# The forget bias of a two-layer attention trunk: four matrix products a head, or a bias tile added by the masking operation

## The chip, the cores and the metric

One core of one Trainium2 chip runs the whole kernel in a single launch. The metric is the device time of that launch in microseconds (us), the median of several executions. TensorE is called PE here, VectorE DVE, ScalarE ACT, GpSimd POOL and SyncE SP; PE's weight loads are PEld.

## The reference

The trunk has two layers over 256 tokens of width 1024. Each layer projects its normalised input and runs three attention branches side by side (MoBA with 6 heads, NSA with 4, FoX with 6, heads of 64), gates them, and projects back. Only the FoX branch matters here. Its logits carry a forget bias, the running sum of a log gate:

```python
log_f = jax.nn.log_sigmoid((ff + b_f)).transpose(0, 2, 1)      # (B, 6 heads, S)
csum = jnp.cumsum(log_f, axis=-1)
s = einsum('bhqd,bhkd->bhqk', q, k) * ATTN_SCALE + cq[..., None] - csum[:, :, None, :]
p = masked_softmax(s, kpos[None, :] <= t[:, None])
```

So each logit of head h gets csum[h, query] - csum[h, key], and keys behind the query's position are masked out.

## The kernel before

The 256 tokens are two tiles of 128. The large products (projections, gates, output) run in three passes on split weights: ACT rounds a staged 128x1024 tile `st` to `wh` (line 275), DVE takes the rest `wl` (line 276), and lines 297 to 299 multiply. Staged tiles have six buffers and split tiles four, so SP loads and ACT/DVE split ahead of PE.

PE's instructions stand in an order that the code writes out itself (`tick`, `unit` and `pairs` weave pieces of attention between the dense products by a clock of their own). The other engines' instructions are put in order by the scheduler of the framework. Each engine then runs its own list strictly in that order and waits on semaphores of the others.

`fz_post` makes the forget sums: a polynomial for the log gate, then three small products with a triangle (lines 880 to 882) that leave csum of the 6 heads on 6 partitions, 256 columns. ACT copies this out (`zf`, line 884), DVE and ACT split it into two parts each of `cpos` and `cneg` (lines 885 to 889), matrices that are zero outside these rows.

`attend` does one head. PE forms the logits of the two query tiles (128 keys for the first, 256 for the second) with two products each (lines 550 and 551). In FoX heads two more products follow for each tile (lines 554 and 555): a column `selr` that picks head h, broadcast, against `cneg`, and `cpos` against the same column. Then DVE adds the mask and takes the row minimum in one operation (line 561, a custom instruction), ACT takes the exponential (line 563), PE transposes (line 568), ACT or DVE copies the transposes out as `pt` (lines 570, 572), and PE multiplies by the values (lines 576 to 580). Heads come in pairs, three FoX pairs a layer. The PSUM tiles `at` of logits, transposes and column layouts share three buffers, so PE's next use of one waits for the engine that reads it last.

Of the kernel before, what the change touches and what calls it, by code (L numbers as in the profile page):

```python
# [9 lines left out]
F32 = mybir.dt.float32  # L10
F32R = mybir.dt.float32r
AF = mybir.ActivationFunctionType
# [6 lines left out]
NT = S // 128  # L19
# [13 lines left out]


K_TRI, K_MASK, K_CMASK, K_CM01 = 0, 128, 384, 448
K_COS, K_SIN, K_CROPE, K_SEL, K_E = 512, 544, 576, 608, 640
K_GCOL, K_PET, K_W2, K_END = 648, 664, 728, 1240

R_G, R_BF, R_NC, R_END = 0, 256, 268, 396

# [1 line left out]
def shape_tables():  # L42
    t = np.arange(S)
    inv = (np.float32(THETA) ** (-np.arange(0, 16, 2, dtype=np.float32) / np.float32(16))).astype(np.float32)

    def rope(pos):
        ang = (pos.astype(np.float32)[:, None] * inv[None, :]).astype(np.float32).astype(np.float64)
        c, s = np.cos(ang), np.sin(ang)
        return (np.concatenate([c, c], 1).astype(np.float32),
                np.concatenate([-s, s], 1).astype(np.float32))  # L50

    k = np.zeros((128, K_GCOL), np.float32)
    i = np.arange(128)
    k[:, K_TRI:K_TRI + 128] = i[:, None] <= i[None, :]
    k[:, K_MASK + 128:K_MASK + 256] = np.where(i[None, :] <= i[:, None], 0.0, NEG)
    end = np.arange(32) * CS + CL - 1
    ok = (end[None, :] <= t[:, None]) & (np.arange(32) < NCMP)[None, :]
    c, s = rope(t)
    for n in range(NT):
        r = slice(n * 128, n * 128 + 128)  # L60
        k[:, K_CMASK + n * 32:K_CMASK + n * 32 + 32] = np.where(ok[r], 0.0, NEG)
        k[:, K_CM01 + n * 32:K_CM01 + n * 32 + 32] = ok[r]
        k[:, K_COS + n * 16:K_COS + n * 16 + 16] = c[r]
        k[:, K_SIN + n * 16:K_SIN + n * 16 + 16] = s[r]
    c, s = rope(end[:NCMP])
    k[:NCMP, K_CROPE:K_CROPE + 16] = c
    k[:NCMP, K_CROPE + 16:K_CROPE + 32] = s
    for kv in range(2):
        for part in range(2):
            for j in range(NCMP):  # L70
                k[(kv * 2 + part) * 16 + j, K_SEL + kv * NCMP + j] = 1.0
    for h in range(FH):
        k[h::32, K_E + h] = 1.0
    return k


# [18 lines left out]
def trunk(ctx, tc, x, w_in, b_gate, cmp_w1, w_up_moba, w_up_nsa, w_up_fox, w_out, first_d, x_t, small_d, row_d, out):  # L95
# [16 lines left out]
    sm = ctx.enter_context(tc.tile_pool(name="sm", bufs=2))  # L112
    pacc = ctx.enter_context(tc.tile_pool(name="pacc", bufs=4, space=PSUM))
    pat = ctx.enter_context(tc.tile_pool(name="pat", bufs=3, space=PSUM))
    po = ctx.enter_context(tc.tile_pool(name="po", bufs=1, space=PSUM))


# [17 lines left out]
    gbc = row[:, R_G:R_BF].rearrange("p (a b) -> p a b", a=16)  # L135
    bfb = row[:, R_BF:R_NC].rearrange("p (l h) -> p l h", l=L)
    ncg = row[:, R_NC:R_END].rearrange("p (l d) -> p l d", l=L)
    selr = const.tile([128, FH], F32R, name="selr")
    cpos = const.tile([128, S], F32R, name="cpos")
    cneg = const.tile([128, S], F32R, name="cneg")  # L140

    klT = {k: const.tile([128, 6, S], F32R, name="klT_" + k) for k in ("mk", "fk")}
    tri = tabs[:, K_TRI:K_TRI + 128]
# [17 lines left out]
    def late_consts():  # L161
        V.memset(ones1, 1.0)
        G.memset(zer, 0.0)
        for s in (0, 64):
            V.memset(gcol[s:s + 16, 0:12], 1.0)
        G.tensor_copy(selr, tabs[:, K_E:K_E + FH])

    def zero_lows():
        for k in klT:
            v = klT[k].rearrange("p (k a) c -> p k a c", a=2)  # L170
            for i in range(2):
                o = slice(64 - i * 64, 128 - i * 64)
                G.tensor_copy(v[o, :, i, :], zer[o][:, :, None].to_broadcast([64, 3, S]))

    def zero_csums():
        G.tensor_copy(cpos, zer.to_broadcast([128, S]))
        G.tensor_copy(cneg, zer.to_broadcast([128, S]))


    nosync = mybir.DependencyInfo(mybir.DependencyClass.NoSync, mybir.DependencyReason.DATA)  # L180
# [181 lines left out]
    def layer(l):  # L362
# [178 lines left out]
        def attend(q, ks, vf, h, bank, hb, rsum, bias=False):  # L541

            wait = in_turn()
            ps = pat.tile([128, 512], F32, name="at")
            p = wk.tile([128, 384], F32, name="p", bufs=4)
            pt = wk.tile([128, 384], F32, name="pt", bufs=3)
            keys = [(t, 128 * (t + 1), ps[:, t * 128:t * 128 + 128 * (t + 1)]) for t in range(NT)]
            for t, nk, sp in keys:
                qs = slice(t * 128, (t + 1) * 128)
                T.matmul(sp, q[:, qs], ks[0][:, 0:nk], start=True, stop=False)  # L550
                T.matmul(sp, q[:, qs], ks[1][:, 0:nk], start=False, stop=not bias)  # L551
                if bias:
                    one = selr[:, h:h + 1]
                    T.matmul(sp, one.to_broadcast([128, 128]), cneg[:, 0:nk], start=False, stop=False)
                    T.matmul(sp, cpos[:, qs], one.to_broadcast([128, nk]), start=False, stop=True)  # L555
                if t < NT - 1:
                    yield None
            for t, nk, sp in keys:
                u = p[:, t * 128:t * 128 + nk]
                nm = sm.tile([128, 1], F32, name="nm", bufs=4)  # L560
                V.tensor_tensor_reduce(out=u, in0=sp, in1=tabs[:, K_MASK + 256 - nk:K_MASK + 256],  # L561
                                       scale=-SCALE, scalar=BIG, op0=ALU.add, op1=ALU.min, accum_out=nm)
                exps.append(A.activation(u, u, AF.Exp, bias=nm, scale=-1.0,  # L563
                                         accum_out=rsum[:, t, hb:hb + 1]))
            yield LAG_S
            pts = pat.tile([128, 512], F32, name="at")
            for s in range(3):
                T.transpose(pts[:, s * 128:(s + 1) * 128], p[:, s * 128:(s + 1) * 128], ident)  # L568
            if h % 2:
                A.activation(pt, pts[:, 0:384], AF.Copy)  # L570
            else:
                V.tensor_copy(pt, pts[:, 0:384])  # L572
            yield LAG_P
            yield from wait(hb == 0)
            bank = bank()
            T.matmul(bank[:, 0, hb, :], pt[:, 0:128], vf(0), start=True, stop=True)
            yield PV
            T.matmul(bank[:, 1, hb, :], pt[:, 128:256], vf(0), start=True, stop=False)
            yield PV
            T.matmul(bank[:, 1, hb, :], pt[:, 256:384], vf(1), start=False, stop=True)  # L580
            turn[1] += 1
# [270 lines left out]
        def fz_post():  # L852
            ps = sh["ps_fz"]
            xf = sm.tile([128, NT, FH], F32, name="xf")
            mn = sm.tile([128, NT, FH], F32, name="mn")
            e = sm.tile([128, NT, FH], F32, name="e")
            d = sm.tile([128, NT, FH], F32, name="d")
            y = sm.tile([128, NT, FH], F32, name="y")
            for t in range(NT):
                V.scalar_tensor_tensor(xf[:, t, :], ps[t][:, 0:FH], sh["r"][:, t:t + 1], bfb[:, l, :],  # L860
                                       op0=ALU.mult, op1=ALU.add)
            V.tensor_scalar(mn, xf, 0.0, None, op0=ALU.min)
            V.scalar_tensor_tensor(e, mn, 2.0, xf, op0=ALU.mult, op1=ALU.subtract)
            exps.append(A.activation(e, e, AF.Exp))
            for t in range(NT):
                evac(ps, t, FH, 384, sh["z"][t][:, 640:1024])

            V.tensor_scalar(d, e, 2.0, None, op0=ALU.add)
            V.reciprocal(d, d)
            V.tensor_tensor(e, e, d, op=ALU.mult)  # L870
            V.tensor_tensor(d, e, e, op=ALU.mult)
            V.tensor_scalar(y, d, 2.0 / 17, 2.0 / 15, op0=ALU.mult, op1=ALU.add)
            for m in (13, 11, 9, 7, 5, 3, 1):
                V.tensor_tensor(y, y, d, op=ALU.mult)
                V.tensor_scalar(y, y, 2.0 / m, None, op0=ALU.add)
            V.tensor_tensor(y, y, e, op=ALU.mult)
            V.tensor_tensor(y, mn, y, op=ALU.subtract)
            yield LAG_F
            ps = pat.tile([128, 512], F32, name="at")
            T.matmul(ps[0:FH, 0:128], y[:, 0, :], tri, start=True, stop=True)  # L880
            T.matmul(ps[0:FH, 128:256], y[:, 0, :], ones1.to_broadcast([128, 128]), start=True, stop=False)
            T.matmul(ps[0:FH, 128:256], y[:, 1, :], tri, start=False, stop=True)
            cs = wk.tile([FH, S], F32, name="zf", bufs=1)
            A.activation(cs, ps[0:FH, 0:S], AF.Copy, scale=1.0 / SCALE)
            V.tensor_copy(cpos[0:FH], cs)
            hi = cpos[0:FH].bitcast(F32)
            V.tensor_tensor(cpos[32:32 + FH], cs, hi, op=ALU.subtract)
            A.activation(cneg[0:FH], hi, AF.Copy, scale=-1.0)
            V.tensor_tensor(cneg[32:32 + FH], hi, cs, op=ALU.subtract)


        def load_gl(c):
# [155 lines left out]
        def run(starts, following):  # L1048
# [9 lines left out]
            mm("mv1")  # L1058
            uv = unit(v_post("mv"))
            if l == 0:  # L1060
                zero_csums()
                zero_lows()
                later_loads()
            mm("b0")
# [94 lines left out]
```

## Time and profile before

| | |
|---|---|
| median of 3 runs | 523.15 us (523.08 to 523.24) |
| profiled execution: its own time | 524.93 us |
| its span, first to last instruction | 522.8 us |
| PE busy | 508.3 us, 97% |
| DVE busy | 395.0 us, 76% |
| ACT busy | 326.3 us, 62% |
| POOL busy | 106.4 us, 20% |
| mean DMA rate | 174 GB/s |

The profiled execution spends 2.1 us outside its span and is 1.8 us above the median; both are kept in mind when a sum is made against it. Busy shares are averages over the whole span and say little about one stage; stretches are read one by one below.

### The profile page before, as it was taken

To read this page: it belongs to the slowest core of one execution; us is meant where nothing else is said; L and a number is where in the kernel's file an instruction comes from. 1 tells how busy PE (TensorE), PEld (TensorE's weight loads), DVE (VectorE), ACT (ScalarE), POOL (GpSimd) and SP (SyncE) were. 2 spreads that over 40 slices of the span, in tenths; PEclk is the share of its full clock that TensorE was granted. 3 is DMA by queue.
4 is the path that set the end of the run, shared out by engine and by line. 5 is a ranking of instruction groups with operands and counts; after the bars stand their busy time and mean duration, and the time that the engine had idled before them with its cause. 6 is when DMAs were issued, how large, how long until landed. Compare 5 with 4: busy or idle time off the path is not lost.

```text
span 522.8 us, 8342 instructions
## 1 busy us (share of the span) xinstructions
PE 508.3 (97%) x2862; PEld 453.4 (87%) x2862; DVE 395.0 (76%) x804; ACT 326.3 (62%) x619; POOL 106.4 (20%) x166
## 2 busy tenths in 40 slices
PE   7999999999999999899999989999999999989997
PEld 4899899999888888788889979999988888878886
DVE  3898787789974558898487987768898754697953
ACT  4886686976584375644276966678756555655440
POOL 3754314000300004025102333030011000132300
PEclk8999999999999999999999989999999999999999
DMA  8998876445554433655447987546437542445502
GB/s 296 334 245 245 234 234 188 141 154 162 173 180 126 147 121 93 205 171 181 136 144 216 226 230 218 178 135 197 158 120 213 170 123 83 160 131 192 180 21 80
DMA packets 56602, 90.73 MB, mean 174 GB/s; under 512 B 3696, under 2 KB 30960, under 8 KB 56560
## 3 DMA queue, kind: packets, MB, share of 16 engines
q1 hardware_dynamic: 55840, 89.08, 56.4%
q10 hardware_dynamic: 720, 1.12, 0.6%
q8 instruction: 22, 0.36, 0.3%
q14 instruction: 20, 0.16, 0.1%
HBM read 89.14 MB, written 1.05 MB: 173 GB/s over the span
## 4 chain that ended last, share of the span: by engine, by line
PE 67%; issue 15%; DVE 7%; POOL 5%; ACT 4%; DMA 1%; ACTq 0%; DVEq 0%; POOLq 0%
PE acc L297 19%; PE acc L299 18%; PE acc L298 18%; DVE wl L276 3%; ACT wh L275 2%; PE at L568 2%; DMA st<-in_w_in_dram 1%; POOL qn L452 1%; DVE om L921 1%; PE at L550 1%; PE at L551 1%; PE at L348 1%; PE at L460 1%; PE o L758 1%; PE o L757 1%
## 5 line engine op out<-in xcount | busy, mean ns | idle before, releaser
L276 DVE TENSOR_TENSOR wl<-st,wh 128x1024 fp32r<-128x1024 f32 (+4 forms) x177 | 201.8, 1147 | 65.3 <-ACT wh L275 63.6
L275 ACT ACTIVATE wh<-st 128x1024 fp32r<-128x1024 f32 (+4 forms) x177 | 169.9, 966 | 98.4 <-PE acc L299 72.0
L297 PE MATMUL acc<-wh,hT 128*128 128x512 f32 (+3 forms) x576 | 223.8, 388 | 2.4 <-ACT wh L275 2.2
L299 PE MATMUL acc<-wh,lT 128*128 128x512 f32 (+3 forms) x576 | 210.4, 365 | 0.0
L298 PE MATMUL acc<-wl,hT 128*128 128x512 f32 (+3 forms) x576 | 209.7, 364 | 0.4 <-DVE wl L276 0.4
L299 PEld LDWEIGHTS acc<-wh,lT 128*128 128x128 f32 x576 | 108.6, 189 | 12.4 <-DVE lT L404 0.9
L297 PEld LDWEIGHTS acc<-wh,hT 128*128 128x128 f32 x576 | 109.4, 190 | 11.0 <-ACT wh L275 2.8
L298 PEld LDWEIGHTS acc<-wl,hT 128*128 128x128 f32 x576 | 109.4, 190 | 8.5 <-DVE wl L276 1.4
L563 ACT ACTIVATE p<-p,nm 128x128 f32<-128x128 f32 x80 | 35.5, 445 | 29.6 <-DVE nm L561 29.5
L920 POOL TENSOR_TENSOR z<-z,tmp 128x512 f32<-128x512 f32 x8 | 13.0, 1653 | 113.2 <-ACT tmp L917 113.2
L561 DVE CUSTOM_DVE_ANT_0 p<-at,tabs 128x128 f32<-128x128 f32 x80 | 24.1, 352 | 9.9 <-PE at L555 9.8
L956 POOL TENSOR_TENSOR mg<-mg,tmp 128x512 f32<-128x512 f32 x8 | 15.8, 1998 | 55.0 <-DVE tmp L955 55.0
L297 PE MATMUL acc<-wh,qkT 128*128 128x512 f32 x64 | 25.2, 394 | 0.0
L299 PE MATMUL acc<-wh,qkT 128*128 128x512 f32 x64 | 24.9, 390 | 0.0
L298 PE MATMUL acc<-wl,qkT 128*128 128x512 f32 x64 | 24.9, 389 | 0.0
L568 PE MATMUL at<-first,p 128*128 128x128 f32 x120 | 19.8, 274 | 0.3 <-ACT qkT L483 0.2
L660 POOL TENSOR_TENSOR om<-om,tmp 128x256 f32<-128x256 f32 x8 | 7.7, 985 | 58.1 <-DVE rs_a L330 50.3
L906 DVE SCALAR_TENSOR_TENSOR gl<-acc,rt,tmp 128x512 f32<-128x512 f32 x24 | 17.0, 743 | 1.1 <-PE o L580 1.1
L568 PEld LDWEIGHTS at<-first,p 128*128 128x128 f32 x120 | 15.0, 146 | 2.5 <-ACT qkT L483 0.6
L758 PE MATMUL o<-wl,Z 128*63 128x256 f32 x64 | 16.3, 289 | 0.9 <-DVE wl L276 0.9
L757 PE MATMUL o<-wh,Z 128*63 128x256 f32 x64 | 16.6, 295 | 0.0
L572 DVE COPY pt<-at 128x384 f32<-128x384 f32 x20 | 11.0, 551 | 7.0 <-PE at L568 6.8
(232 smaller groups left out, 710.0 us busy)
## 6 DMA issues: line engine op xcount, KB each, us to landing
st<-in_w_in_dram SPq DMA_DIRECT2D x54, 512.0 KB, 3.4
st<-in_w_in_dram SPq DMA_DIRECT2D x56, 384.0 KB, 3.9
st<-in_cmp_w_dram SPq DMA_DIRECT2D x32, 256.0 KB, 4.2
st<-in_w_out_dram SPq DMA_DIRECT2D x16, 512.0 KB, 3.8
st<-in_w_in_dram SPq DMA_DIRECT2D x8, 396.0 KB, 6.9
st<-in_w_in_dram SPq DMA_DIRECT2D x8, 390.0 KB, 3.3
tmp<-in_b_gate_dram SPq DMA_DIRECT2D x12, 256.0 KB, 4.4
st<-in_w_up_moba_dram SPq DMA_DIRECT2D x4, 512.0 KB, 3.7
```

Source lines behind the costliest of these rows:

```text
L275: A.activation(h, sv[:, i:i + m], AF.Copy)
L276: V.tensor_tensor(w_["l"][:, i:i + m], sv[:, i:i + m], h.bitcast(F32), op=ALU.subtract)
L297: T.matmul(ps, sh, wh, start=first, stop=False)
L298: T.matmul(ps, sh, wl, start=False, stop=False)
L299: T.matmul(ps, sl, wh, start=False, stop=last)
L561: V.tensor_tensor_reduce(out=u, in0=sp, in1=tabs[:, K_MASK + 256 - nk:K_MASK + 256], scale=-SCALE, scalar=BIG, op0=ALU.add, op1=ALU.min, a ...
L563: exps.append(A.activation(u, u, AF.Exp, bias=nm, scale=-1.0, accum_out=rsum[:, t, hb:hb + 1]))
L568: T.transpose(pts[:, s * 128:(s + 1) * 128], p[:, s * 128:(s + 1) * 128], ident)
L757: T.matmul(U, st, h, start=i == 0, stop=False)
L758: T.matmul(U, st, lo, start=False, stop=i == CL - 1)
L906: V.scalar_tensor_tensor(sh["gl"][t][b][:, n * 512:(n + 1) * 512], ps[t], sh["r"][:, t:t + 1], bg, op0=ALU.mult, op1=ALU.add)
L956: (G if b == 1 else V).tensor_tensor(m, m, tmp, op=ALU.add)
```

## The change

The two extra products for each tile are gone, and with them `selr`, `cpos`, `cneg` and the steps that made them. Instead, ACT scales the 6x256 sums twice (negative and positive), writes them to a buffer in device memory (`csd`), and loads them back from there: once spread over all 128 partitions as key rows (`ck`, two transfers of 128x6x128 and 128x6x256 numbers), and once with queries on the partitions (`cq`, two transfers of 128x6 single numbers). POOL adds the causal mask to the two diagonal blocks of `ck` for all heads at once. For each head and query tile ACT makes a bias tile from `ck` plus the query's own sum (an Identity activation with a bias column), and the masking operation of DVE reads this tile in place of the mask.

```diff
+            if bias:
+                both = wk.tile([128, 384], F32, name="bias", bufs=3)
+                for t, nk, _ in keys:
+                    add[t] = both[:, t * 128:t * 128 + nk]
+                    A.activation(add[t], sh["ck"][:, h, t * 128:t * 128 + nk], AF.Identity, bias=sh["cq"][:, t, h:h + 1])
...
                 T.matmul(sp, q[:, qs], ks[0][:, 0:nk], start=True, stop=False)
-                T.matmul(sp, q[:, qs], ks[1][:, 0:nk], start=False, stop=not bias)
-                if bias:
-                    one = selr[:, h:h + 1]
-                    T.matmul(sp, one.to_broadcast([128, 128]), cneg[:, 0:nk], start=False, stop=False)
-                    T.matmul(sp, cpos[:, qs], one.to_broadcast([128, nk]), start=False, stop=True)
+                T.matmul(sp, q[:, qs], ks[1][:, 0:nk], start=False, stop=True)
...
-                V.tensor_tensor_reduce(out=u, in0=sp, in1=tabs[:, K_MASK + 256 - nk:K_MASK + 256],
+                V.tensor_tensor_reduce(out=u, in0=sp, in1=add[t],
...
-            cs = wk.tile([FH, S], F32, name="zf", bufs=1)
-            A.activation(cs, ps[0:FH, 0:S], AF.Copy, scale=1.0 / SCALE)
-            V.tensor_copy(cpos[0:FH], cs)
-            hi = cpos[0:FH].bitcast(F32)
-            V.tensor_tensor(cpos[32:32 + FH], cs, hi, op=ALU.subtract)
-            A.activation(cneg[0:FH], hi, AF.Copy, scale=-1.0)
-            V.tensor_tensor(cneg[32:32 + FH], hi, cs, op=ALU.subtract)
+
+            cs = wk.tile([FH, 2, S], F32, name="cs", bufs=1)
+            for i in range(2):
+                A.activation(cs[:, i, :], ps[0:FH, 0:S], AF.Copy, scale=(2 * i - 1) / SCALE)
+            csd = dram.tile([FH, 2, S], F32, name="csd")
+            sh["ck"] = lay.tile([128, FH, 384], F32, name="ck")
+            sh["cq"] = lay.tile([128, NT, FH], F32, name="cq")
+            nc.scalar.dma_start(csd, cs)
+            nc.scalar.dma_start(sh["ck"][:, :, 0:128], csd[:, 0, 0:128][None].to_broadcast([128, FH, 128]))
+            nc.scalar.dma_start(sh["ck"][:, :, 128:384], csd[:, 0, :][None].to_broadcast([128, FH, S]))
+            for t in range(NT):
+                nc.scalar.dma_start(sh["cq"][:, t, :], csd[:, 1, t * 128:(t + 1) * 128].rearrange("h q -> q h"))
+            mask = tabs[:, K_MASK + 128:K_MASK + 256][:, None, :].to_broadcast([128, FH, 128])
+            for i in (0, 256):
+                G.tensor_tensor(sh["ck"][:, :, i:i + 128], sh["ck"][:, :, i:i + 128], mask, op=ALU.add)
...
-        G.tensor_copy(selr, tabs[:, K_E:K_E + FH])
...
-                zero_csums()
```

The changed program's lines are numbered differently (the exponential of line 563 is its line 556, the split of 275 its 266); names with a number are buffers. PE's list is the old one with the 48 rows of lines 554 and 555 taken out and nothing else moved. Two places on ACT and one on POOL differ in more than that; the second layer repeats them.

On ACT, where the forget sums leave PSUM in the first layer, there stood before (`uc` is NSA's compressed branch, `rs_y` a normalisation, `p` the exponentials of the first MoBA pair):

```order
L884 ACTIVATE zf_1718<-at_1714 6x256
L830 ACTIVATE uc_1675<-uc_1675 128x128
L275 ACTIVATE wh_1730<-st_1728 128x1024
L327 ACTIVATE rs_y_1693<-rs_v_1692 128x2x6
L888 ACTIVATE cneg_100<-cpos_99 6x256
L328 ACTIVATE rs_y_1693<-rs_y_1693 128x2x6
L563 ACTIVATE p_1752,rsum_1750<-p_1752,nm_1763 128x128
```

In the changed program the same place, up to the same exponential, reads:

```order
L879 ACTIVATE cs_1714<-at_1710 6x256 x2
L883 DMA csd_1717<-cs_1714 6x512
L823 ACTIVATE uc_1671<-uc_1671 128x128
L318 ACTIVATE rs_y_1689<-rs_v_1688 128x2x6
L266 ACTIVATE wh_1733<-st_1731 128x1024
L319 ACTIVATE rs_y_1689<-rs_y_1689 128x2x6
L884 DMA ck_1718<-csd_1717 128x6x128
L885 DMA ck_1718<-csd_1717 128x6x256
L887 DMA cq_1719<-csd_1717 128x6x1 x2
L556 ACTIVATE p_1755,rsum_1753<-p_1755,nm_1766 128x128
```

Five transfer issues have come in; the four loads stand behind a wait for the store to land, and the exponentials of the first MoBA pair stand behind the four loads.

A little later on ACT, between the last exponential of the first MoBA pair and the first of the second, there stood before:

```order
L563 ACTIVATE p_1757,rsum_1750<-p_1757,nm_1774 128x256
L275 ACTIVATE wh_1811<-st_1809 128x1024
L275 ACTIVATE wh_1885<-st_1883 128x1024
L570 ACTIVATE pt_1758<-at_1843 128x384
L563 ACTIVATE p_1849,rsum_1750<-p_1849,nm_1861 128x128
```

and now stands:

```order
L266 ACTIVATE wh_1788<-st_1786 128x1024
L266 ACTIVATE wh_1814<-st_1812 128x1024
L266 ACTIVATE wh_1888<-st_1886 128x1024
L544 ACTIVATE bias_2084<-ck_1718,cq_1719 128x128
L563 ACTIVATE pt_1761<-at_1846 128x384
L544 ACTIVATE bias_2084<-ck_1718,cq_1719 128x256
L544 ACTIVATE bias_2092<-ck_1718,cq_1719 128x128
L544 ACTIVATE bias_2092<-ck_1718,cq_1719 128x256
L544 ACTIVATE bias_2155<-ck_1718,cq_1719 128x128
L544 ACTIVATE bias_2155<-ck_1718,cq_1719 128x256
L556 ACTIVATE p_1852,rsum_1753<-p_1852,nm_1864 128x128
```

Six bias tiles, for the first three of the six FoX heads, now stand there, one ahead of the copy `pt` and five between it and the next exponentials. The other six stand later, in front of the second and third FoX pair.

On POOL, in the same stretch, the second pair of NSA sums `om` stood before behind the first and one fill:

```order
L660 TENSOR_TENSOR om0_115<-om0_115,tmp_1744 128x256
L660 TENSOR_TENSOR om1_116<-om1_116,tmp_1747 128x256
L803 MEMSET vcb_3854 128x256
L660 TENSOR_TENSOR om0_115<-om0_115,tmp_1837 128x256
L660 TENSOR_TENSOR om1_116<-om1_116,tmp_1840 128x256
```

and now has the two mask additions ahead of it:

```order
L653 TENSOR_TENSOR om0_114<-om0_114,tmp_1747 128x256
L653 TENSOR_TENSOR om1_115<-om1_115,tmp_1750 128x256
L890 TENSOR_TENSOR ck_1718<-ck_1718,tabs_96 128x6x128 x2
L796 MEMSET vcb_3851 128x256
L653 TENSOR_TENSOR om0_114<-om0_114,tmp_1840 128x256
L653 TENSOR_TENSOR om1_115<-om1_115,tmp_1843 128x256
```

The first addition waits for the smaller transfer of `ck`, the second for the larger. The first bias tile on ACT waits for the first addition and the first transfer of `cq`, the second for the second addition and the second transfer of `cq`.

## Rows read from the trace of the kernel before

**Rows 1.** The page's head: span, then busy time (share) and instructions of PE.

```profile
span 522.8 us, 8342 instructions
PE 508.3 (97%) x2862; PEld 453.4 (87%) x2862; DVE 395.0 (76%) x804; ACT 326.3 (62%) x619; POOL 106.4 (20%) x166
```

**Rows 2.** Stretches: length, busy PE, PEld, DVE, ACT, POOL, clock, DMA, GB/s.

```profile
140.00:142.00 2.00, 2.00 (x15) 1.78 (x15) 2.00 (x4) 0.40 (x1) 1.52 (x2) 1.00 0.96 332
162.00:183.00 21.00, 21.00 (x137) 18.74 (x136) 10.35 (x31) 9.61 (x25) 0.00 (x0) 1.00 0.41 127
308.00:310.00 2.00, 1.68 (x7) 1.58 (x8) 0.90 (x2) 0.76 (x3) 0.25 (x1) 0.59 1.06 229
```

**Rows 3.** PE's waits in the whole span: us in total, times, longest.

```profile
PE at L348 <- DVE qkT L354: 3.2, 2, 1.6
PE at L460 <- POOL qn L452: 2.7, 4, 1.3
```

**Rows 4.** PE in order of time: start, us; a MoBA pair's logits, then a FoX pair's.

```profile
139.63 0.30 PE L550 MATMUL at<-qkT 128*128 128x128 f32 x1
...
140.63 0.39 PE L297 MATMUL acc<-wh,hT 128*128 128x512 f32 x1
...
161.95 0.31 PE L550 MATMUL at<-qkT 128*128 128x128 f32 x1
...
163.84 0.39 PE L297 MATMUL acc<-wh,hT 128*128 128x512 f32 x1
```

**Rows 5.** Line 554 (line 555 likewise): ns (min/median/max), first and last start.

```profile
L554 PE MATMUL at<-cneg,selr x24: 273/276/281, 162.2 to 438.5; 128*128 128x128 f32 x12, 128*128 128x256 f32 x12
```

**Rows 6.** ACT in order of time where the sums leave PSUM.

```profile
127.43 0.38 ACT L884 ACTIVATE zf<-at 6x256 f32<-6x256 f32 x1
...
129.69 0.20 ACT L328 ACTIVATE rs_y<-rs_y 128x12 f32<-128x12 f32 x1
132.76 0.40 ACT L563 ACTIVATE p<-p,nm 128x128 f32<-128x128 f32 x1 [2.87 <-DVE nm L561]
```

**Rows 7.** Issue times of loads on ACT's queue, ns (min/median/max).

```profile
L256 ACTq DMA_DIRECT2D st<-in_w_in_dram x4: 452/453/631, 1.2 to 2.6; - x4
```

**Rows 8.** Transfers: count, KB each, median us from issue to landing.

```profile
st<-in_w_in_dram SPq DMA_DIRECT2D x54, 512.0 KB, 3.4
...
out_dram<-x SPq DMA_DIRECT2D x2, 128.0 KB, 1.7
```

**Rows 9.** DMA from 158 to 160 us, while one b_gate load runs alone.

```profile
DMA packets 158, 0.29 MB, mean 145 GB/s; under 512 B 16, under 2 KB 16, under 8 KB 158
```

**Rows 10.** Line 897 (b_gate spread over 128 partitions, 256 KB): issue to landing.

```profile
DMA to landing us min/median/max: 3.2/4.4/5.2
```

**Rows 11.** DMA from 16 to 20 us, when many loads run at once.

```profile
DMA packets 1031, 1.50 MB, mean 376 GB/s; under 512 B 60, under 2 KB 1031, under 8 KB 1031
```

**Rows 12.** POOL's additions of 256 and 512 columns, ns (min/median/max).

```profile
L660 POOL TENSOR_TENSOR om<-om,tmp x8: 736/740/1721, 131.7 to 397.4; 128x256 f32<-128x256 f32 x8
L920 POOL TENSOR_TENSOR z<-z,tmp x8: 1301/1744/1827, 199.5 to 460.5; 128x512 f32<-128x512 f32 x8
```

**Rows 13.** ACT in order of time from the last split to the column layouts.

```profile
138.72 1.06 ACT L275 ACTIVATE wh<-st 128x1024 fp32r<-128x1024 f32 x1 [1.75 <-PE acc L299]
139.91 0.49 ACT L570 ACTIVATE pt<-at 128x384 f32<-128x384 f32 x1
142.55 0.40 ACT L563 ACTIVATE p<-p,nm 128x128 f32<-128x128 f32 x1 [2.15 <-DVE nm L561]
```

**Rows 14.** Line 563: exponentials of 128 and 256 columns, ns (min/median/max).

```profile
L563 ACT ACTIVATE p<-p,nm x80: 383/448/510, 91.6 to 440.2; 128x128 f32<-128x128 f32 x40, 128x256 f32<-128x256 f32 x40
```

**Rows 15.** PE's next uses of a freed PSUM buffer, in order of time.

```profile
141.32 0.49 PE L460 MATMUL at<-first,qn 128*128 128x128 f32 x3
...
149.13 0.50 PE L568 MATMUL at<-first,p 128*128 128x128 f32 x3
```

**Rows 16.** DVE in order of time: the copy that frees the buffer.

```profile
147.78 0.56 DVE L572 COPY pt<-at 128x384 f32<-128x384 f32 x1
```

More of the change, by code (lines that the diff above doesn't have):

```diff
@@ L35 @@
 K_TRI, K_MASK, K_CMASK, K_CM01 = 0, 128, 384, 448
-K_COS, K_SIN, K_CROPE, K_SEL, K_E = 512, 544, 576, 608, 640
-K_GCOL, K_PET, K_W2, K_END = 648, 664, 728, 1240
+K_COS, K_SIN, K_CROPE, K_SEL = 512, 544, 576, 608
+K_GCOL, K_PET, K_W2, K_END = 640, 656, 720, 1232
 R_G, R_BF, R_NC, R_END = 0, 256, 268, 396
@@ L71, in shape_tables @@
                 k[(kv * 2 + part) * 16 + j, K_SEL + kv * NCMP + j] = 1.0
-    for h in range(FH):
-        k[h::32, K_E + h] = 1.0
     return k
@@ L114, in trunk @@
     pat = ctx.enter_context(tc.tile_pool(name="pat", bufs=3, space=PSUM))
+    dram = ctx.enter_context(tc.tile_pool(name="dram", bufs=2, space=bass.MemoryType.DRAM))
     po = ctx.enter_context(tc.tile_pool(name="po", bufs=1, space=PSUM))
@@ L137, in trunk @@
     ncg = row[:, R_NC:R_END].rearrange("p (l d) -> p l d", l=L)
-    selr = const.tile([128, FH], F32R, name="selr")
-    cpos = const.tile([128, S], F32R, name="cpos")
-    cneg = const.tile([128, S], F32R, name="cneg")
     klT = {k: const.tile([128, 6, S], F32R, name="klT_" + k) for k in ("mk", "fk")}
@@ L173, in zero_lows @@
                 G.tensor_copy(v[o, :, i, :], zer[o][:, :, None].to_broadcast([64, 3, S]))
-    def zero_csums():
-        G.tensor_copy(cpos, zer.to_broadcast([128, S]))
-        G.tensor_copy(cneg, zer.to_broadcast([128, S]))
     nosync = mybir.DependencyInfo(mybir.DependencyClass.NoSync, mybir.DependencyReason.DATA)
@@ L547, in attend @@
             keys = [(t, 128 * (t + 1), ps[:, t * 128:t * 128 + 128 * (t + 1)]) for t in range(NT)]
+            add = [tabs[:, K_MASK + 256 - nk:K_MASK + 256] for _, nk, _ in keys]
+            if bias:
[3 more added lines that the diff above has]
+                    A.activation(add[t], sh["ck"][:, h, t * 128:t * 128 + nk], AF.Identity, bias=sh["cq"][:, t, h:h + 1])
             for t, nk, sp in keys:
@@ L1150 @@
     arrays = {f"in_{n}_dram": np.ascontiguousarray(a) for n, a in lay_out(inputs).items()}
-    nc = bacc.Bacc("TRN2", target_bir_lowering=False, num_devices=1)
+    nc = bacc.Bacc("TRN2", target_bir_lowering=False, num_devices=1, dynamic_dma_scratch_size=2048)
     args = [nc.dram_tensor(n, a.shape, mybir.dt.from_np(a.dtype), kind="ExternalInput").ap()
```

## The prediction

> **What bounds the kernel now.** I read the page's head first: PE is busy for 508.3 of 522.8 us [rows 1]. That is an average, so I looked at the stretches the change touches. While the dense products and FoX pairs run, from 162 to 183 us, PE is busy for every microsecond at the full granted clock, and ACT for 9.61 of 21 [rows 2]. PE's list of waits shows why nothing else bounds it: over the whole span its largest waits are 3.2 and 2.7 us, at other places than these [rows 3]. So PE's list decides: work taken out of it is gained, unless an engine that PE waits for comes later than it does now. Time in order shows what an added pair of products costs there: a MoBA pair's logits take from 139.63 to 140.63, 1.00 us, a FoX pair's from 161.95 to 163.84, 1.89 us [rows 4].
>
> **What is removed.** Per head four products go, 48 in all, 24 on each line, about 0.27 us each by the row, but they overlap in the pipeline [rows 5]. The honest price is the pair's difference: 1.89 - 1.00 = 0.89 us. Six pairs give 5.3 us, and they are gained because PE never waits in that stretch [rows 2]. The three DVE steps and one ACT step that made `cpos` and `cneg`, and POOL's fills at the start, go too. I count 0 for them: PE's waits do not name them [rows 3].
>
> **What is added, in the first layer (the second repeats it; times on the clock of before).** The sums leave PSUM at 127.43 [rows 6].
> - Two scalings of 0.38 in place of one end near 128.2 [rows 6]. The issue of the store takes 0.45 [rows 7], and a small store lands 1.7 after it [rows 8]: near 130.3. ACT meanwhile does the work that it has anyway, up to the `rs_y` of 129.69 [rows 6].
> - Four loads, each 0.45 to 0.63 of issue [rows 7], are out between 132.1 and 132.8. The next exponential starts at 132.76, after 2.87 of idling [rows 6]. The idle time covers the issues: 0. Without that cover they would cost 1.8 to 2.5 a layer.
> - The broadcasts bring 128x6x128 and 128x6x256 numbers, 0.39 and 0.79 MB, in 768 pieces each. A lone broadcast moves 145 GB/s [rows 9], so 2.7 and 5.4 us; its landing of 3.2 [rows 10] less the 1.8 that 0.26 MB need at this pace leaves 1.4 fixed. From 130.3: landed at about 134.4 and 139.8.
> - The two transfers of `cq` come behind them in the same queue. Each consists of 768 single numbers of 4 bytes. No row of before shows such pieces. Their bounds: 0 if bytes set the pace, 9.7 us each if pieces do at the lone broadcast's pace of 158 in 2 us [rows 9]. Between them stands the pace under many loads: 1031 packets in 4 us, 258 a microsecond [rows 11], which is 3.0 us for 768. I take it, since a queue with its transfers waiting one behind the other is more like that stretch than like one transfer alone, and the engines have company too: SP's loads hold 0.96 of them from 140 to 142 [rows 2]. So `cq` lands at 142.8 and 145.8.
> - POOL adds the mask to 768 columns twice. From 740 for 256 columns and 1744 for 512, a 768-column one is 2.75 us; from the minima 736 and 1301, 1.9 [rows 12]. I take 2.4: done at 136.8 and 142.2.
>
> The GPSIMD Engine Reference of the Trainium skill (section "3.1 Elementwise — side-by-side cycle accounting") gives 4497 ns for a 2048-column float32 addition; scaled to 768 that is an estimate of 1.7 us, below the rows here, and it would put the second addition at 141.5, too early to matter either way.
>
> **Who waits.** ACT's list now holds, behind the split that ends at 139.8 [rows 13], the first bias tile, `pt`, and five more bias tiles, then the exponentials of the next MoBA pair. The first bias tile waits for the first addition and the first `cq`, the second for the second of both. An engine runs strictly in order, so what stands behind is late with them:
> - `pt` frees the PSUM buffer that PE needs at 141.32 [rows 15]. `pt` takes 0.49 [rows 13] and a bias tile I price like an exponential, 0.38 to 0.51 [rows 14]. With `cq` at 142.8 `pt` ends near 143.7 and PE stands for 2.4 us.
> - The five tiles take about 2.1 us [rows 14]. From 145.8 they end at 147.9, where the exponential that started at 142.55 [rows 13] can begin. ACT is dense from there on, and DVE, whose copy of 147.78 frees the buffer [rows 16] for PE at 149.13 [rows 15], follows ACT's steps. That copy ends at 148.34: slack 0.79. So the second bias tile may begin at 142.55 + 0.79 - 2.1, about 141.3, without harm; at 145.8 PE is 4.5 us late, the 2.4 from above within it.
> - Two layers: 9.0 us. The bias tiles of the later pairs, two pairs of four a layer, fall into ACT's idle share of 162 to 183 [rows 2]: 0.
>
> From 308 to 310 us, where PE stands idle for 0.32 of 2 us, the granted clock is 0.59, the 1.2 GHz level or near it; in the busy stretches it is 1.00 [rows 2]. A stall of 4.5 us could bring such a fall on as well; two microseconds at 0.59 are 0.8 us of lost work, 1.5 in the whole kernel. I keep it for the upper end, with 0 at the lower.
>
> **The sum.** The profiled execution takes 524.93 with a span of 522.8 [rows 1], and lies 1.8 above the median. 524.93 - 5.3 + 9.0 = 528.6; against the median, 523.15 - 5.3 + 9.0 = 526.9 us. The range of this case alone: `cq` done from 144.4 to 148 (pieces up to a third slower, as they share engines with SP's loads) is 524.0 to 531.2.
>
> The DMA page of the Trainium skill (DMA: Bandwidth & Descriptors, section "Rules for kernel authors") speaks against this change: a strided last dimension turns into one descriptor per element. That is the layout of `cq`, 128 queries out of rows of 256. It agrees with my choice of counting pieces and gives no pace; no row of before shows one.
>
> **Rivals.**
> - *Small stall, faster.* Single numbers cost little, and `cq` lands with the second broadcast near 140 to 142. Then POOL's second addition at 142.2 is last: 0.9 a layer, 523.15 - 5.3 + 1.8 = 519.6 (518.2 to 522). For it: two transfers of 3 KB are few bytes. Against it: 1536 pieces behind 1536 others.
> - *No stall, the whole gain.* Broadcasts faster than 145 GB/s (the loads reach 376 [rows 11]) and the short addition: the second tile begins before 141.3, 517.8 us. Against it: the lone broadcast's row.
> - *The stall eats the gain.* Stalls of 2.1 to 3.2 a layer, 522.1 to 524.2: `cq` done from 143.4 to 144.5. From 144.0 on the kernel is slower; this is the point that decides.
> - *All pieces at the lone pace.* Four transfers of 9.7 from 131.7 on end at 170.5, even behind PE's first FoX pair [rows 4]; the second tile 29 us late in each layer, some 575 us. With only `cq` at that pace, 159.2 and 554 us. Against it: that row [rows 9] is one transfer's latency as much as its pace.
> - *The gain is not there*, because the products were covered by something else, at which PE would now wait. Against it: no wait of PE in the stretch and an ACT half idle [rows 2]; it falls to the third case.
>
> **Numbers.** Forecast (4.5 a layer) 0.40; small stall 0.24; whole gain 0.14; gain eaten 0.13; lone pace or worse 0.09. A difference of 0.2%, 1.05 us, is about what a measurement of this kernel can tell. Faster gets the second and third and a little of the fourth, 0.40; same 0.10; slower 0.50. The range leaves out the whole gain's lower part and the lone pace: 517.9 to 531.5.
>
> **What would show it.** PE's count falls from 2862 to 2814, and a FoX pair's logits take 1.0 us. ACT idles ahead of the first and second bias tile of a layer, released by a DMA of `cq` (forecast) or by POOL's addition of `ck` (small stall), or not at all. The landing of the four loads, and POOL's 768-column addition, test the chain's terms one by one. PE's waits should show one at the column layouts near 141 and one at a transpose near 149, and the clock behind them whether it fell. I am wrong if `cq` lands before 143, or if PE's stall is far from what ACT is late beyond 141.3, which would mean that my slack is mis-read; the product saving is wrong if the time gained between stalls is not 5.3.

## The result and the profile after

The changed kernel takes 519.55 us (median of 6 runs, 518.66 to 521.3) against 523.19 for the kernel before (6 runs, 523.05 to 524.51): a ratio of 0.9931, 95% interval 0.991 to 0.9951. It is faster by 3.6 us. The forecast was 526.9, slower; the measured time is that of the first rival, "small stall, faster", worked out at 519.6, though its stall came about in another way than that rival had it.

The page's head of the changed kernel, to be held against [rows 1]:

```profile
span 519.5 us, 8277 instructions
...
PE 504.0 (97%) x2814; PEld 449.0 (86%) x2814; DVE 395.6 (76%) x798; ACT 334.4 (64%) x643; POOL 114.6 (22%) x167
```

The span is 3.3 us shorter and PE has its 48 instructions less. PE in order of time, changed kernel, first layer (start, length; in brackets the idle time ahead of it and what ended it):

```profile
139.48 0.30 PE L547 MATMUL at<-qkT 128*128 128x128 f32 x1
...
142.37 0.55 PE L451 MATMUL at<-first,qn 128*128 128x128 f32 x3 [1.02 <-ACT pt L563]
...
163.19 0.31 PE L547 MATMUL at<-qkT 128*128 128x128 f32 x1
...
164.21 0.39 PE L288 MATMUL acc<-wh,hT 128*128 128x512 f32 x1
```

A FoX pair's logits take 164.21 - 163.19 = 1.02 us, where they took 1.89 [rows 4]. But the pair starts 1.24 later than before, although the MoBA pair's logits at 139.48 were 0.15 early: 1.4 us have been lost between, and the one wait with a name there is for `pt`, as in the wait list of the whole span:

```profile
PE at L451 <- POOL qn L443: 2.7, 4, 1.3
...
PE at L451 <- ACT pt L563: 1.7, 2, 1.0
```

ACT in the same stretch, changed kernel (ACTq is a transfer issued from ACT):

```profile
130.40 0.56 ACTq L885 DMA_DIRECT2D ck<-csd  x1
131.00 2.61 ACTq L887 DMA_DIRECT2D cq<-csd  x2
133.66 0.40 ACT L556 ACTIVATE p<-p,nm 128x128 f32<-128x128 f32 x1 [3.70 <-DVE rr L322]
...
138.57 1.06 ACT L266 ACTIVATE wh<-st 128x1024 fp32r<-128x1024 f32 x1 [0.56 <-PE acc L290]
141.53 0.40 ACT L544 ACTIVATE bias<-ck,cq 128x128 f32<-128x128 f32 x1 [1.90 <-DMA cq<-csd]
141.84 0.47 ACT L563 ACTIVATE pt<-at 128x384 f32<-128x384 f32 x1
142.62 1.90 ACT L544 ACTIVATE bias<-ck,cq 128x256 f32<-128x256 f32 x5 [0.31 <-POOL ck L890]
144.43 0.39 ACT L556 ACTIVATE p<-p,nm 128x128 f32<-128x128 f32 x1
```

The chain stands where it was forecast, with one number changed. The first bias tile waits for `cq` until 141.53 and holds `pt`, and this is the wait that PE shows. Before, the column layouts started 1.69 us behind the MoBA pair's first logits (139.63 to 141.32, [rows 4] and [rows 15]), and now 2.89 behind them (139.48 to 142.37): 1.20 of the 1.4 us are lost here. The second bias tile waits 0.31 more for POOL's second addition, until 142.62, and not for `cq`. POOL's two additions there:

```profile
135.62 1.86 POOL L890 TENSOR_TENSOR ck<-ck,tabs 128x768 f32<-128x768 f32 x1 [2.08 <-DMA ck<-csd]
139.78 2.81 POOL L890 TENSOR_TENSOR ck<-ck,tabs 128x768 f32<-128x768 f32 x1 [2.29 <-PE at L561]
```

In the second layer POOL's second addition is done before the second bias tile's turn comes, and only the first tile waits. POOL, ACT and PE there:

```profile
394.37 2.02 POOL L890 TENSOR_TENSOR ck<-ck,tabs 128x768 f32<-128x768 f32 x1 [2.36 <-DMA ck<-csd]
```

```profile
396.04 0.40 ACT L544 ACTIVATE bias<-ck,cq 128x128 f32<-128x128 f32 x1 [1.54 <-DMA cq<-csd]
396.34 0.47 ACT L563 ACTIVATE pt<-at 128x384 f32<-128x384 f32 x1
396.71 1.89 ACT L544 ACTIVATE bias<-ck,cq 128x256 f32<-128x256 f32 x5
```

```profile
394.34 0.30 PE L547 MATMUL at<-qkT 128*128 128x128 f32 x1
...
396.87 0.55 PE L451 MATMUL at<-first,qn 128*128 128x128 f32 x3 [0.66 <-ACT pt L563]
```

From the logits to the column layouts PE needs 2.53 us here and needed 1.70 before (395.88 to 397.58): 0.83 is lost, again behind `pt` and `cq`.

DVE's list has changed as well. Two of its splits (line 276, now 267), which stood at 135.17 and 137.00 before, now stand together behind DVE's copy `pt`, where POOL's second addition meets them:

```profile
138.56 2.35 DVE L267 TENSOR_TENSOR wl<-st,wh 128x1024 fp32r<-128x1024 f32 x2
```

The landing times of the larger broadcast (line 885), then those of the two `cq` transfers of the first layer, changed kernel:

```profile
DMA to landing us min/median/max: 9.1/9.2/9.3
```

```profile
DMA to landing us min/median/max: 10.0/10.2/10.4
```

The broadcast issued at 130.40 lands near 139.7; the `cq` transfers, issued at 131.00 and about 131.6, near 141.4 and 141.6. The 1536 single numbers came in within 2 us of the broadcast.

A running difference tells where time went better than any total. The table takes from each kernel's PE timeline the distance between the first logits of the second and of the third MoBA pair, 12.73 us in the kernel before (139.63 to 152.36, and 395.88 to 408.62 in the second layer). What a kernel has beyond that is its stall in that layer.

| kernel | first layer | second layer | median, us | ratio to before (95%) |
|---|---|---|---|---|
| changed | 1.38 | 0.90 | 519.55 | 0.9931 (0.991 to 0.9951) |
| e1_cq_rows | 0.43 | 0.42 | 518.75 | 0.9914 (0.9899 to 0.9928) |
| e2_late | 0.00 | 0.50 | 519.08 | 0.9913 (0.9898 to 0.9928) |
| e3_no_bias | 0.02 | 0.02 | 517.56 | 0.9893 (0.9876 to 0.991) |
| e4_kept | 1.00 | 0.81 | 525.67 | 1.0042 (1.003 to 1.0053) |
| e5_ck_only | 1.43 | 1.34 | 520.86 | 0.9955 (0.994 to 0.9971) |
| e7_no_add | 0.00 | 0.00 | 517.67 | 0.989 (0.9873 to 0.9907) |
| e8_adds_late | 0.03 | 0.03 | 517.99 | 0.9889 (0.9873 to 0.9904) |

One thing is needed to read spans of single executions: near 306 us, between the layers, PE waits for other reasons, and in some of the profiles, though not in all, the clock falls behind that wait. e7_no_add has the fall and e8_adds_late has not; their stalls are the same and their spans 517.5 and 515.9. Their edits differ too, but the executions of e7_no_add alone lie from 517.54 to 519.26, so some 1.6 us of a span can be the fall and no edit's work. The clock (third number from the end of a row) in the changed kernel,

```profile
306.00:308.00 2.00, 1.24 (x5) 1.15 (x5) 1.15 (x3) 0.95 (x2) 0.69 (x4) 0.69 1.08 262
308.00:310.00 2.00, 2.00 (x11) 1.93 (x10) 0.92 (x2) 1.52 (x3) 0.00 (x0) 0.50 1.08 223
```

as in [rows 2], and in the profile of e8_adds_late:

```profile
308.00:310.00 2.00, 2.00 (x14) 2.00 (x13) 2.00 (x5) 1.46 (x4) 0.00 (x0) 1.00 1.12 223
```

The stalls of the table lie away from it, within one layer, and are free of this.

### The profile page after: what moved, and what is told of

Read it like the earlier page. It is cut to its first block, busy times and chain, and to the rows that moved or that the text cites. A ratio compares the mean times of both kernels' runs of the same rounds, so it can differ in the third digit from the quotient of the medians.

```text
span 519.5 us, 8277 instructions
## 1 busy us (share of the span) xinstructions
PE 504.0 (97%) x2814; PEld 449.0 (86%) x2814; DVE 395.6 (76%) x798; ACT 334.4 (64%) x643; POOL 114.6 (22%) x167
## 4 chain that ended last, share of the span: by engine, by line
PE 65%; issue 15%; DVE 7%; POOL 5%; ACT 4%; DMA 3%; ACTq 0%; DVEq 0%; POOLq 0%
PE acc L288 18%; PE acc L290 17%; PE acc L289 17%; DVE wl L267 3%; DMA cq<-csd 2%; ACT wh L266 2%; PE at L561 1%; POOL qn L443 1%; DVE om L922 1%; PE at L451 1%; PE at L339 1%; PE at L547 1%; PE o L751 1%; DMA st<-in_w_in_dram 1%; PE at L548 1%
## 5 line engine op out<-in xcount | busy, mean ns | idle before, releaser
L554 DVE CUSTOM_DVE_ANT_0 p<-at,tabs 128x128 f32<-128x128 f32 (+1 forms) x56 | 17.1, 352 | 0.1
L451 PE MATMUL at<-first,qn 128*128 128x128 f32 x64 | 12.1, 280 | 4.5 <-POOL qn L443 2.7
```

What stands on the lines that cost most here:

```text
L451: T.transpose(p3[:, k, :], qf[:, k * 128:(k + 1) * 128], ident)
L554: V.tensor_tensor_reduce(out=u, in0=sp, in1=add[t], scale=-SCALE, scalar=BIG, op0=ALU.add, op1=ALU.min, accum_out=nm)
```

## The experiments

**e1_cq_rows: `cq` in longer pieces.**

```diff
-                nc.scalar.dma_start(sh["cq"][:, t, :], csd[:, 1, t * 128:(t + 1) * 128].rearrange("h q -> q h"))
...
+                nc.scalar.dma_start(sh["cq"][:, t, :], flat[:, t * FH:(t + 1) * FH])
```

`flat` is `csd` seen as 128 rows of 24 numbers.

> The two cq transfers read 24 bytes in one piece for each partition instead of six single numbers (128 pieces of 24 bytes in place of 768 of 4, so the values are not the query's sums). Theory: after the change POOL's second addition is what the second bias tile waits for in the first layer (the trace of the changed kernel: that tile starts at 142.62, released by POOL), and the 4-byte pieces cost about 1 us a transfer. Then the wait of PE at the column layouts goes away in both layers, but the first layer stays about 1.3 us late because of POOL, the second about 0.6: some 0.3 us faster than the changed kernel, about 519.2 us. Rival (my forecast's step): the 4-byte pieces are the slow part at 3 us a transfer; then both layers win more than 1 us and the time falls to about 517.3 us.

Measured 518.75 us. ACT in order of time:

```profile
139.75 0.40 ACT L544 ACTIVATE bias<-ck,cq 128x128 f32<-128x128 f32 x1 [0.17 <-DMA cq<-csd]
140.06 0.47 ACT L563 ACTIVATE pt<-at 128x384 f32<-128x384 f32 x1
141.45 1.89 ACT L544 ACTIVATE bias<-ck,cq 128x256 f32<-128x256 f32 x5 [0.92 <-POOL ck L891]
143.41 0.40 ACT L556 ACTIVATE p<-p,nm 128x128 f32<-128x128 f32 x1
```

The first bias tile comes 1.8 us earlier (141.53 to 139.75). Some 0.3 of it is the broadcast ahead, after which POOL starts at 139.50 instead of 139.78; the rest, 1.5 us, is what the single numbers of the first transfer cost beyond longer pieces. The second transfer gains less: it is issued near 131.6 and lands 9.3 later, near 140.9, which is 1.4 behind the broadcast where the single numbers took 1.9. So the number of pieces is only a part of what these transfers cost. PE's wait at the column layouts is gone in both layers, so it was the time of `cq` that made it. Still the second tile waits for POOL, in both layers, and some stall stays. The theory holds for the order of things and not for its size: the first layer's stall fell to 0.43, not 1.3, because POOL's second addition took 1.92 here instead of 2.81. It began a little earlier, and now DVE pays:

```profile
138.51 3.99 DVE L267 TENSOR_TENSOR wl<-st,wh 128x1024 fp32r<-128x1024 f32 x2
```

The two splits take 3.99 instead of 2.35, and DVE masks the second MoBA pair from 143.09 on instead of 141.49. The exponential of 143.41 needs that too, so the 0.43 left cannot be put down to the second bias tile alone. The rival's 517.3 is not reached.

**e2_late: the bias tiles elsewhere in ACT's list.**

```diff
-                    A.activation(add[t], sh["ck"][:, h, t * 128:t * 128 + nk], AF.Identity, bias=sh["cq"][:, t, h:h + 1])
+                    i = A.activation(add[t], sh["ck"][:, h, t * 128:t * 128 + nk], AF.Identity, bias=sh["cq"][:, t, h:h + 1])
+                    after(i, exps[-1:])
```

> The same work, only ACT's order is changed: each bias tile stands behind the last exponential recorded before it, so behind the MoBA pairs. Theory: all of what the change gives back (2.3 us in two layers) is the place of the bias tiles in ACT's list; the transfers and POOL then have some 15 us more and nothing waits: 523.2 - 5.3 = 517.9 us at most, by the profiled gain 2.3 below the changed kernel, about 517.3 us. Rival: the transfers themselves cost time (shared with the weight loads, or the issue on ACT's queue), or the bias tiles delay the FoX pairs instead: 519 us or more.

Measured 519.08 (517.78 to 519.65), with a profiled span of 517.9, 1.6 under that of the changed kernel; both have the clock's fall. By the median it is the rival's 519 that came, and the interval overlaps that of the changed kernel; the traces divide the two. The first layer's stall is gone with not one transfer changed, so there it was the place in the list. The second layer keeps 0.50, without a bias tile in front of anything: the theory was not the whole. DVE's two splits beside POOL's second addition take 3.99 us in that layer and 2.35 in the first.

**e3_no_bias: only the removal.** The edit drops the chain and the bias tiles from the changed kernel.

> The forget bias is left out altogether: no extra products, no transfers, no POOL additions, no bias tiles, FoX heads masked like the others. Theory: the removal of the 48 products is worth 0.89 us a pair, 5.3 us: 517.9 us, or about 517.2 by the profiled run. Rival: the removal is worth less (the difference of 3.6 us between the two kernels is all there is), 519.5 us; or more, below 516.5, which would mean that the stall is larger than 2.3 us.

Measured 517.56 us and no stall. The products, with the small steps that fed them, are worth 523.13 - 517.56 = 5.6 us in medians; the forecast's term was 5.3.

**e4_kept: only the chain.**

```diff
...
+                    one = zt[:, 0:1]
+                    T.matmul(sp, one.to_broadcast([128, 128]), one.to_broadcast([128, nk]), start=False, stop=False)
+                    T.matmul(sp, zt, one.to_broadcast([128, nk]), start=False, stop=True)
...
```

> The changed kernel with 48 extra products put back, on a tile of zeros that adds nothing: the chain of the change without its saving. Theory: saving and stall add up, so this is 5.3 us above the changed kernel and 1.5 to 2.5 us above the kernel before: about 525 us. Rival: PE has slack in the FoX stretch in the changed kernel, the products are partly hidden: 522 us or less.

Measured 525.67 us: 2.5 above before (1.6 to 2.8 by the interval), with stalls of 1.00 and 0.81. Within this, saving and stall add up as two terms. ACT in the first layer:

```profile
141.36 0.40 ACT L545 ACTIVATE bias<-ck,cq 128x128 f32<-128x128 f32 x1 [1.65 <-DMA cq<-csd]
141.67 0.47 ACT L568 ACTIVATE pt<-at 128x384 f32<-128x384 f32 x1
142.04 1.88 ACT L545 ACTIVATE bias<-ck,cq 128x256 f32<-128x256 f32 x5
```

The second bias tile waits for nothing here, in either layer: POOL's second addition took 1.90 and was done at 141.53. The first tile's wait for `cq` makes this stall without POOL.

**e5_ck_only: no query term, no bias tiles.**

```diff
-                both = wk.tile([128, 384], F32, name="bias", bufs=3)
-                for t, nk, _ in keys:
-                    add[t] = both[:, t * 128:t * 128 + nk]
-                    A.activation(add[t], ...)
+                add = [sh["ck"][:, h, t * 128:t * 128 + nk] for t, nk, _ in keys]
...
-            for i in (0, 256):
-                G.tensor_tensor(sh["ck"][:, :, i:i + 128], sh["ck"][:, :, i:i + 128], mask, op=ALU.add)
+            for i, j in ((0, 128), (256, 256)):
+                G.tensor_tensor(sh["ck"][:, :, i:i + 128], sh["ck"][:, :, j:j + 128], mask, op=ALU.add)
```

> The query's own sum is left out of the logits: it is the same number for all keys of a row, so the softmax takes it out again. With it go both cq transfers, the positive sums and all 24 bias tiles on ACT; the masking operation reads ck itself. One broadcast of 128x6x256 in place of two; POOL writes the masked copy of the diagonal block. Theory (the loss is ACT's bias tiles waiting in the middle of its list): nothing is left that waits, the full 5.3 us: about 517.5 us, the FoX pairs of the first layer at their old start, and at most the 0.5 us of the second layer lost that the run with late bias tiles still showed beside POOL's additions. Rival (the transfers or POOL's additions cost PE time by themselves): 518.5 us or more.

Measured 520.86 us, no faster than the changed kernel (1.3 above in medians, with intervals that overlap), with less work on ACT and in the queue. Both parts of the theory fell: the stalls are 1.43 and 1.34, and the rival's 518.5 or more came, by POOL's additions. POOL and DVE in order of time show what came in their place:

```profile
134.56 4.62 POOL L882 TENSOR_TENSOR ck<-ck,tabs 128x768 f32<-128x768 f32 x2 [1.56 <-DMA ck<-csd]
```

```profile
135.00 2.50 DVE L267 TENSOR_TENSOR wl<-st,wh 128x1024 fp32r<-128x1024 f32 x1
137.41 0.47 DVE L829 COPY pc<-at 128x128 f32<-128x128 f32 x2
137.81 2.46 DVE L267 TENSOR_TENSOR wl<-st,wh 128x1024 fp32r<-128x1024 f32 x1
140.19 0.54 DVE L562 COPY pt<-at 128x384 f32<-128x384 f32 x1
```

With one broadcast the two additions follow each other, beside two of DVE's splits, and each split takes 2.5 us; beside an idle POOL it takes 1.2 (129.79 in the same timeline: 1.23). DVE's `pt` copy comes at 140.19, 2.3 us later than in e8_adds_late (137.87), and PE waits for it at the logits. The lengths fit engines that take turns: from 134.56, one addition of 1.86, one split of 1.2, an addition and a split again would end at 136.4, 137.6, 139.5 and 140.7; the splits ended at 137.50 and 140.27 and the second addition at 139.18, within 0.4 of that. This is a reading of the rows; no run tests it by itself.

**e6_cq_thrice: four more `cq` transfers ahead of the two.** Their target is an unused tile.

```diff
...
+            for t in range(2 * NT):
+                nc.scalar.dma_start(sh["cx"][:, t, :], csd[:, 1, t % 2 * 128:(t % 2 + 1) * 128].rearrange("h q -> q h"))
```

> Four more cq transfers of 768 single numbers stand ahead of the two real ones. Theory (about 770 single numbers a microsecond, as the changed kernel's landings suggest): the real ones land some 4 us later, near 145.5 in the first layer, and the bias tiles and what stands behind them with them: 2.5 to 4 us a layer more than the changed kernel, 525 to 528 us. Rival (258 a microsecond, the pace of my forecast): 12 us later, 540 us or more. Third: the issue of each transfer holds ACT until the one before is nearly done; then the exponentials behind the issues start several us late, which the first logits' transposes show first.

Measured 535.8 us, ratio 1.0227 (1.021 to 1.0243). The third way came true. ACT in order of time:

```profile
130.98 8.44 ACTq L888 DMA_DIRECT2D cx<-csd  x4
139.45 2.17 ACTq L890 DMA_DIRECT2D cq<-csd  x2
141.66 0.40 ACT L556 ACTIVATE p<-p,nm 128x128 f32<-128x128 f32 x1 [11.65 <-DMA cx<-csd]
```

The issues hold ACT for 10.6 us, and PE waits 6.1 for the exponentials, at the transposes. The clock then shows the 1.2 GHz level:

```profile
142.00:144.00 2.00, 1.77 (x5) 1.33 (x6) 0.56 (x1) 2.00 (x9) 0.00 (x0) 0.50 0.36 3
144.00:146.00 2.00, 2.00 (x6) 1.57 (x5) 0.01 (x1) 1.42 (x2) 0.00 (x0) 0.50 0.00 0
```

From the first to the second MoBA pair the layer takes 18.05 us instead of 9.54, 8.5 late, of which the wait is 6.1; the rest, 2.4, fits some 4.7 us at half the clock behind it. The loss lies ahead of the distance that the table reads, so this kernel has no row there. As to the pace: the second `cq` is issued at 141.1 and lands 2.9 us later, near 144.0. The larger broadcast landed near 138.7, so six transfers took 5.3 us, 0.9 each, 870 numbers a microsecond. The forecast's 258 a microsecond would have made 18 us of them.

**e7_no_add: e2_late without POOL's additions.**

```diff
...
-            for i in (0, 256):
-                G.tensor_tensor(sh["ck"][:, :, i:i + 128], sh["ck"][:, :, i:i + 128], mask, op=ALU.add)
```

> The run with late bias tiles, without POOL's two mask additions (the FoX heads then lack the causal mask in the diagonal blocks). Theory: while POOL adds 768 columns, DVE's split operations take 2 us instead of 1.2, and that is the 0.5 us which the second layer still loses with late bias tiles; without the additions DVE's splits go back to 1.2 us there, the 0.5 us are gone, and the whole gain of 5.3 us is left: about 517.4 us. Rival: DVE is late for its own order; then the 0.5 us stay.

Measured 517.67 us, and no stall in either layer. The second layer's half microsecond of e2_late came from POOL's additions.

**e8_adds_late: e5_ck_only with the additions later.** They are recorded with the first FoX head and ordered behind the last exponential before it.

```diff
+                if h == 0:
...
+                    for i, j in ((0, 128), (256, 256)):
+                        o = G.tensor_tensor(sh["ck"][:, :, i:i + 128], sh["ck"][:, :, j:j + 128], mask, op=ALU.add)
+                        after(o, exps[-1:])
```

> As the run without cq and bias tiles, with POOL's additions held until the last exponential ahead of the FoX heads, where DVE has idle time. Theory: no wait of the change is left in either layer, 5.3 us under the kernel before or a little more: about 517.3 us, and the second layer's FoX pairs start without loss. Rival: the additions are now too late for the first masking operation of a FoX pair: PE waits at its transposes, 518 us or more.

Measured 517.99 us (517.82 to 518.14), ratio 0.9889 (0.9873 to 0.9904). The additions stand at 142.60 now, behind POOL's NSA sums and away from the two splits, and the stalls are 0.03. Between e5_ck_only and this kernel nothing but the place of two POOL instructions a layer differs, and it is worth 2.9 us in medians. It is 1.6 us under the changed kernel and level with e3_no_bias, which has no bias at all.

## Why the prediction was wrong

**The saving was right.** 0.89 us a pair and 5.3 in all were forecast; the pair's 1.02 us shows it, and e3_no_bias alone gives 5.6. PE was the bound.

**The slack was right, as far as the runs can tell.** The forecast let the second bias tile begin at 141.3 without harm. The changed kernel runs 0.15 early there, so its limit is 141.15; the tile began at 142.62, 1.47 past it, and the stall is 1.38. In e1_cq_rows: 141.45 against a limit of 141.1, 0.35, and 0.43 measured. Neither is a clean test: in the changed kernel 1.20 of the 1.38 had been lost at the column layouts already, and in e1_cq_rows DVE is late as well.

**The larger broadcast and POOL were right to half a microsecond.** The larger broadcast landed near 139.7 (forecast 139.8), the second addition ended at 142.6 (142.2), at 2.81 for itself where 2.4 was taken. The smaller broadcast landed near 135.5 instead of 134.4; POOL was idle afterwards, so nothing came of it.

**The step that failed is the price of the `cq` transfers**: "1031 packets in 4 us, 258 a microsecond [rows 11], which is 3.0 us for 768. I take it". They landed near 141.4 and 141.6 instead of 142.8 and 145.8: 1 us each on average, and 0.9 in e6_cq_thrice. The row that was chosen has packets of some 1.5 KB (1.50 MB in 1031) and moved 376 GB/s; it had told the pace of bytes, which bounds the pace of pieces from below only. So the wait that was forecast came, and was smaller. `cq` held the first bias tile and `pt`, and PE lost 1.20 and 0.83 us at the column layouts where 2.4 were forecast; that is most of the stalls of 1.38 and 0.90. What did not come is the second tile's wait for the second `cq`, from which the 4.5 us a layer were made: that tile waited 0.31 for POOL in the first layer and for nothing in the second.

**The small-stall rival hit its number by luck.** It had `cq` landing from 140 to 142, which is right, and made its 0.9 a layer of POOL's second addition alone. By the forecast's own sum for `pt`, `cq` at 141.4 already costs about 1.0 us: `pt` ends at 142.3, and PE needs it at 141.32. e4_kept has stalls of 1.00 and 0.81 without any wait for POOL. With 2.3 instead of 9.0 the forecast's sum is 523.15 - 5.3 + 2.3 = 520.2.

**Two steps held by luck.** The four load issues were priced at 0.45 to 0.63 each, and at nothing in the sum: "The idle time covers the issues: 0". The second `cq` issue alone took 2.0 us (2.61 for the two), and the first exponential came at 133.66 instead of 132.76; PE did not notice. e6_cq_thrice shows the price without the cover. And POOL's additions were counted only as a link in the chain; e5_ck_only and e7_no_add show that they also slow DVE. In the changed kernel the larger part of the loss is ACT's list all the same: e2_late moves the bias tiles (and, by the scheduler, one copy `qkT`, ahead of three of the exponentials) and wins 1.38 in the first layer and 0.40 of 0.90 in the second; what is left there goes with the additions in e7_no_add.

**The rule of the Trainium skill** that was weighed (DMA: Bandwidth & Descriptors, "Rules for kernel authors": a strided last dimension becomes one descriptor per element) agrees with e1_cq_rows in its direction: the same bytes in longer pieces came 1.5 us earlier for the first transfer, beyond the broadcast's share, and 0.5 for the second. But a rule without a pace did not decide the case.

**The clock's upper end was not needed here.** The wait of 1.02 in the changed kernel left the granted clock at 1.00 through 142 to 148 us. The 6.1 us of e6_cq_thrice did not. In the kernel before, more idle time lies ahead of the row that the forecast took [rows 2] than in it: PE is busy for only 0.85 of the 2 us from 306 to 308.

**Two slips in the sums change nothing.** The range ends at 531.2 where it is worked out and at 531.5 where it is stated. And a second addition that is done at 141.5 would not be quite too early to matter, since the limit was put at 141.3.

## What to carry to other kernels

Price small transfers by a row that counts pieces of their size, or say that the rows give only one side; a busy stretch of large packets says little about how fast small ones can go. Work that is added to an engine with idle time is still placed in a list: look at what stands behind it and when its input lands, for the first such wait as well as for the last, and order it behind the last thing that must not wait. And ask of an added POOL instruction not only when it ends, but which DVE instruction runs beside it.

## What the runs showed of the hardware beyond what was expected

- A transfer's issue can hold its engine: 0.55 us for the third load in ACT's queue, 2.0 for the fourth (1.8 with the longer pieces of e1_cq_rows), and 8.44 for four in a row when broadcasts and single numbers were still queued ahead.
- DVE's 128x1024 subtraction takes 1.2 us beside an idle POOL and 2.5 us beside POOL's 128x768 addition; that addition itself took from 1.80 to 2.83 us. In these traces the one that starts second is the one that takes longer: POOL in the changed kernel's first layer (2.81, and 2.35 for the two splits), DVE in e1_cq_rows (1.92, and 3.99 for the two splits).
- A wait of PE of 1.0 us left the clock at 1.00; one of 6.1 us, which ended at 142.2, left it at 0.50 until 146 us and at 0.81 from 146 to 148.
